# Tail tiles of four batches, seeded dots and one last store in a record-counting kernel

## The chip, the cores and the metric

The kernel runs on one core of a Trainium2 chip. The metric is the device time of one execution in microseconds (us).

Engines: DVE is VectorE, ACT is ScalarE, Pool is GpSimd, PE is TensorE, SP is SyncE (here it only issues transfers).

## The reference

```
x: (8, 2048, 4096) float32      w: (4096, 1) float32
proj = (x @ w).squeeze(-1)                      # (8, 2048)
cm = np.maximum.accumulate(proj, axis=1)
is_record = (proj >= cm).astype(np.float32)
return np.cumsum(is_record, axis=1)             # (8, 2048) float32
```

x is 268 MB and each element is used once.

## The kernel before

Positions 0 to 1919 are done in four groups. A group takes eight tiles, one for each batch, of 128 partitions with 4, 4, 4 and then 3 rows of x each. Of every row, DVE multiplies and sums 2816 columns (one custom instruction, "dot"); Pool multiplies the other 1280 and ACT sums these. The sum of a dot is written out by a second instruction, the "read-out". PE turns the sums into an (8, positions) layout, and DVE runs scan, compare and scan on it (running maximum, comparison with it, running count). The last 128 positions of all batches are the tail, in eight tiles (numbered 0 to 7) of 64 positions of 2 batches; tiles 6 and 7 are cut into column pieces, so that little work is left after the last landing. A tail tile holds several batches in its 128 partitions; "masking" multiplies its sums by a 0/1 pattern of the batches, so that a matmul puts each sum in the row of its batch.

```
H = 2; Q = P // H                  # batches in a tail tile, positions in it
LAST = [(B-2, 1696, D, (1696, VC), (VC, D)), (B-2, 0, 1696, (0, 1696), None),
        (B-1, 2592, D, (2592, CV), (CV, D)), ..., (B-1, 352, 736, (352, 736), None),
        (B-1, 0, 352, (0, 352), None)]      # tile, columns loaded, DVE's, Pool's

def dot(xsl, wsl, dst):
    return V.tensor_tensor_reduce(out=xsl, in0=xsl, in1=wsl, scale=1.0, scalar=0.0,
                                  op0=ALU.mult, op1=ALU.add, accum_out=dst)

def group_dots(r, g=0):                               # DVE
    for t in range(B):
        if r == R:
            V.wait_ge(xs[t], 16).then_inc(go, 1)      # landed: DVE tells Pool
        for j in range(r):
            i = dot(...)
            if j == 0 and r < R:
                i._wait_ge(xs[t], 16).then_inc(go, 1) # last group
            elif j == 1:
                i.then_inc(xs[t], -16)
# [cut] Pool: first product of each tile waits for go >= 1

# the end of the tail
for j in range(NP):
    sums(i, accs[:, j:j+1], accs[:, NP+j:NP+j+1])     # five pieces of tile 7
V.wait_ge(pa, na)
V.tensor_reduce(out=fin, in_=accs, op=ALU.add, ...)   # add the pieces' sums
by_batch(B-1, fin, False, True, sd, nv).then_inc(psr, 1)   # mask on DVE, matmul
tail_scans(EARLY, B, ...)                             # last 64 positions
SY.dma_start(out=out[:, S0:], in_=cnt_l)._wait_ge(cs, NG+3).then_inc(oe, 16)
G.wait_ge(oe, 16 * 2)                                 # Pool waits for both stores
```

The last group's 384 columns are stored earlier, from the middle of the load queue; `cnt_l` holds the tail's 128 columns, 4 KB.

Of the kernel before, what the change touches and what calls it, by code (L numbers as in the profile page):

```python
# [20 lines left out]
def kernel(  # L21
# [16 lines left out]
    P = 128  # L38
# [17 lines left out]
    H = 2  # L56
    Q = P // H
    LAST = [
        (B - 2, 1696, D, (1696, VC), (VC, D)),
        (B - 2, 0, 1696, (0, 1696), None),  # L60
        (B - 1, 2592, D, (2592, CV), (CV, D)),
        (B - 1, 1440, 2592, (1792, 2592), (1440, 1792)),
        (B - 1, 736, 1440, (736, 1280), (1280, 1440)),
        (B - 1, 352, 736, (352, 736), None),
        (B - 1, 0, 352, (0, 352), None),
    ]
    def rows_of(m):
        return m * H % B, m * H // B * Q

    TILES = [(m, 0, D, (0, VC), (VC, D)) for m in range(B - 2)] + LAST  # L70
    NP = sum(q[0] == B - 1 for q in LAST)
    EARLY = 4
    W2, W2C = 1280, WC
# [10 lines left out]
    small = sb([P, 352], "small")  # L84
    w2 = sb([P, W2C], "w2")
    xall = sb([P, NS * R * D], "xall")
# [4 lines left out]
    masked = sb([P, 2 * P], "masked")  # L91
    fold = sb([P, 2 * B - H + Q], "fold")
    cm_l, cnt_l = (sb([B, P], n) for n in ("cm_l", "cnt_l"))
# [3 lines left out]
    by_b, by_i = fold[:, : 2 * B - H], fold[:, 2 * B - H :]  # L97
# [3 lines left out]
    def cut(n):  # L101
        off[0] += n
        assert off[0] <= 352
        return small[:, off[0] - n : off[0]]

    sum_v, sum_p = cut(R * B), cut(R * B)
    acc_v, acc_p = cut(B + 1), cut(B)
    accs = cut(2 * NP)
    fin = cut(1)
# [4 lines left out]
    def sem(name):  # L114
# [5 lines left out]
    ws, bw, wc, cs, od, oe, psr, pd, pl, go, sd, pa, con, fo, ms, p7, mg = (  # L120
        sem(n) for n in "ws bw wc cs od oe psr pd pl go sd pa con fo ms p7 mg".split()
# [4 lines left out]
    def dot(xsl, wsl, dst):  # L126
        return V.tensor_tensor_reduce(  # L127
            out=xsl, in0=xsl, in1=wsl, scale=1.0, scalar=0.0,
            op0=ALU.mult, op1=ALU.add, accum_out=dst,
        )  # L130
# [35 lines left out]
    with tc.tile_critical(no_gpsimd_drain=True):  # L166
# [30 lines left out]
        for i, (m, c0, c1, _, _) in enumerate(TILES):  # L197
# [11 lines left out]
            if i == len(TILES) - 4:  # L209
                SY.dma_start(  # L210
                    out=out[:, STARTS[-1] : S0], in_=cnt[:, : S0 - STARTS[-1]]
                )._wait_ge(cs, NG + 1).then_inc(oe, 16)
# [9 lines left out]
        G.memset(by_b, 0.0).then_inc(con, 1)  # L222
# [5 lines left out]
        for n, k in enumerate(order):  # L228
# [17 lines left out]
            out=by_b[:, B - H : B], in_=identity.rearrange("p (i b) -> p b i", b=H),  # L246
# [12 lines left out]
        def group_dots(r, g=0):  # L259
            for t in range(B):  # L260
                b, xb = B - 1 - t, at(g, t)
                if r == R:
                    V.wait_ge(xs[t], 16).then_inc(go, 1)
                for j in range(r):
# [4 lines left out]
                    if j == 0 and r < R:  # L269
                        i._wait_ge(xs[t], 16).then_inc(go, 1)  # L270
                    elif j == 1:
                        i.then_inc(xs[t], -16)
# [10 lines left out]
        def group_products(r, g=0):  # L283
            for t in range(B):
                for j in range(r):
                    xl = at(g, t)[:, j * D + VC : (j + 1) * D]
                    i = G.tensor_mul(out=xl, in0=xl, in1=w_sb).then_inc(pl, 1)  # L287
                    if j == 0:
                        i._wait_ge(go, 1)
                G.sem_inc(go, -1)  # L290

        G.wait_ge(wc, 3)
        with G.Fori(0, NL):
            group_products(R)
        group_products(RS[-1], NL)
# [17 lines left out]
        def group_rows(r):  # L313
            T.wait_ge(fr[B - 1], 2).then_inc(p7, 1)
            T.sem_inc(fr[B - 1], -2)
            T.wait_ge(od, 16).then_inc(od, -16)  # L316
# [14 lines left out]
        nv = npool = na = nm = on_a = on_g = 0  # L331

        def sums(i, dst_v, dst_p):
# [3 lines left out]
            dot(xb[:, v[0] : v[1]], w_v[:, v[0] : v[1]], dst_v)._wait_ge(  # L337
# [12 lines left out]
        def by_batch(m, acc, start, stop, *wait):  # L350
            nonlocal nm, on_a, on_g
            e = masked[:, nm * B : (nm + 1) * B]
            b, q = rows_of(m)
            on = by_b[:, B - H - b : 2 * B - H - b]
            pool = m < B - 2 and wait[0] is sd
            if pool:
                G.tensor_tensor(
                    out=e, in0=on, in1=acc.to_broadcast([P, B]), op=ALU.mult
                )._wait_ge(*wait).then_inc(mg, 1)
            elif m < B - 1:  # L360
                A.activation(out=e, in_=on, func=ACTF.Copy, scale=acc)._wait_ge(  # L361
                    *wait
                ).then_inc(ms, 1)
            else:
                V.tensor_tensor(  # L365
                    out=e, in0=on, in1=acc.to_broadcast([P, B]), op=ALU.mult
                )._wait_ge(*wait).then_inc(ms, 1)
            nm += 1
            if pool:
                on_g += 1  # L370
            else:
                on_a += 1
            return T.matmul(  # L373
                out=ps[:B, q : q + Q], lhsT=e, rhs=by_i, start=start, stop=bool(stop),
            )._wait_ge(*((mg, on_g) if pool else (ms, on_a)))

        def tail_scans(m0, m1, cm0, cnt0, base):
            a, b = (m * H * Q // B for m in (m0, m1))
            scans(cm_l[:, a:b], cnt_l[:, a:b], ps[:B, a:b], cm0, cnt0, base)

        n = RS[-1] * P
        for i, (m, c0, _, _, p) in enumerate(TILES[: -NP]):
            dv = acc_v[:, i : i + 1]
            sums(i, dv, acc_p[:, m : m + 1])
            if m in (0, EARLY):
                T.wait_ge(cs, NG + 1 + (m > 0))
            if p:
                by_batch(m, acc_p[:, m : m + 1], rows_of(m)[0] == 0, False, pa, na)
# [50 lines left out]
```

## Time and profile before

| | before |
|---|---|
| time, median of 3 runs | 630.22 us (630.19 to 630.41) |
| span of the profiled run | 628.8 us |
| busy: DVE, Pool, ACT, PE | 65%, 59%, 29%, 5% |
| load queue's share of 16 DMA engines' span | 98.9% |
| HBM read | 268.45 MB, 427 GB/s over the span |

These are the page's lines on the DMA engines: busy tenths in 40 slices of the span, GB/s in the same slices, the load queue with its share of 16 engines' span, and the chain of waits by engine.

```profile
DMA  9999999999999999999999999999999999999996
GB/s 401 400 467 400 467 400 467 401 463 404 463 404 463 404 463 404 464 404 463 404 463 404 463 404 467 400 464 404 467 417 444 407 450 441 411 450 441 405 424 248
...
q1 hardware_dynamic: 6560, 268.50, 98.9%
...
POOL 52%; issue 38%; DMA 6%; PE 2%; DVE 1%; SPq 0%; POOLq 0%; ACT 0%; ACTq 0%
```

The DMA engines are 90% busy or more until the last slice. The GB/s line swings from slice to slice; the trace's packets are up to 64 KB long, but whether that is why was not tested. A full tile of 8.39 MB lands every 19.3 us, which is 435 GB/s. The Trainium skill, page "DMA: Bandwidth & Descriptors", section Specifications, gives 435 GB/s as the ceiling of the fabric; this trace sits on it. So the kernel is bound by its load stream, and only what lies before and after that stream can be saved. The chain's "POOL 52%" is no limit: the chain is followed back from tile to tile through whichever engine released the next step, while Pool itself is idle 41% of the span.

This is the end of the timeline of the kernel before: start in us, duration in us, engine, line, operation, output and inputs, shapes, and in brackets how long the engine was idle and what ended that.

```profile
623.39 0.55 DVE L127 CUSTOM_DVE_ANT_0 xall<-xall,w_v 128x384 f32<-128x384 f32 x1
...
623.87 0.52 DVE L127 CUSTOM_DVE_ANT_0 xall<-xall,w_v 128x352 f32<-128x352 f32 x1
624.31 0.08 DVE L127 DVE_READ_ACCUMULATOR2_ANT small<- 128x1 f32 x1
624.43 0.16 DVE L400 TENSOR_REDUCE small<-small 128x1 f32<-128x10 f32 x1
624.62 0.17 DVE L365 TENSOR_TENSOR masked<-fold,small 128x8 f32<-128x8 f32 x1
...
624.85 0.38 PE L373 MATMUL ps<-fold,masked 128*8 128x64 f32 x2 [2.46 <-DVE masked L365]
625.27 0.34 DVE L143 TENSOR_TENSOR_SCAN cm_l<-ps,cm_l,small 8x64 f32<-8x64 f32 x1 [0.48 <-PE ps L373]
625.64 0.22 DVE L146 TENSOR_TENSOR ps<-ps,cm_l 8x64 f32<-8x64 f32 x1
625.89 0.34 DVE L149 TENSOR_TENSOR_SCAN cnt_l<-ps,cnt_l,small 8x64 f32<-8x64 f32 x1
626.26 0.31 SPq L407 DMA_DIRECT2D out_dram<-cnt_l  x1
```

Read it as a chain without gaps: two last dots (384 and 352 columns), the second's read-out at 624.31, the reduce, the masking of the sums by batch, a matmul (which these traces record as two), scan, compare and scan over 64 positions, the store's issue at 626.26. No dot waits for a landing here: DVE is slightly late. From the store's issue to the end of the span, 2.56 us, no engine computes. (The page rounds spans to 0.1 us; the traces hold 628.817 for this kernel, and the times counted from an event below use the traces' nanoseconds, so they can differ by 0.01 from what the lines shown give.)

The DMA view of the same kernel, GB/s in 40 slices of 0.125 us from 625 to 630 us, shows that store's data: one slice.

```profile
GB/s 0 0 0 0 0 0 0 0 0 0 0 0 0 0 0 0 33 0 0 0 0 0 0 0 0 0 0 0 0 0 0 0 0 0 0 0 0 0 0 0
```

And two lines of its timeline from the last group of full tiles show when the two engines begin one and the same tile.

```profile
584.40 3.09 DVE L127 CUSTOM_DVE_ANT_0 xall<-xall,w_v 128x2816 f32<-128x2816 f32 x1 [5.41 <-DMA xall<-in_x_dram]
...
587.57 8.63 POOL L287 TENSOR_TENSOR xall<-xall,w_sb 128x1280 f32<-128x1280 f32 x3 [5.91 <-POOLq L290]
```

DVE begins on the landing, Pool 3.17 us later: there `go` is raised by DVE's first dot when it is done. In the groups of four rows DVE raises it by a separate wait, before the dot, and Pool begins with DVE.

### The profile page before, as it was taken

What the parts mean: (1) busy time and instruction counts of PE and PEld (TensorE: products, weight loads), DVE (VectorE), ACT (ScalarE), POOL (GpSimd) and SP (SyncE); (2) the same over time, 40 slices, a digit from 0 to 9 for tenths busy, and PEclk for the clock granted to TensorE, in tenths of its full rate; (3) what the DMA queues carried; (4) which work ended last, traced back from release to release, by engine and by line L of the source; (5) the groups of instructions that cost most, each with busy time, mean ns of one, the idle gap of its engine ahead of it and who ended that gap; (6) DMA issues with size and microseconds to landing.
All of it is one profiled execution on the core that took longest, in us unless ns stands there. A gap on an engine that the chain in (4) does not pass through costs nothing.

```text
span 628.8 us, 1182 instructions
## 1 busy us (share of the span) xinstructions
PE 31.7 (5%) x108; PEld 15.0 (2%) x108; DVE 406.9 (65%) x292; ACT 180.4 (29%) x273; POOL 369.9 (59%) x147
## 2 busy tenths in 40 slices
PE   8000000000010000000010000000002000000031
PEld 3000000000010000000010000000001000000010
DVE  0755776556785557755579555676556966655897
ACT  1222332223322233222233222332223232232353
POOL 0555676446765557745567555676555666666685
PEclk9999999999965555555555555555555555555555
DMA  9999999999999999999999999999999999999996
GB/s 401 400 467 400 467 400 467 401 463 404 463 404 463 404 463 404 464 404 463 404 463 404 463 404 467 400 464 404 467 417 444 407 450 441 411 450 441 405 424 248
DMA packets 6579, 268.55 MB, mean 427 GB/s; under 512 B 768, under 2 KB 1040, under 8 KB 1584
## 3 DMA queue, kind: packets, MB, share of 16 engines
q1 hardware_dynamic: 6560, 268.50, 98.9%
q10 hardware_dynamic: 16, 0.02, 0.0%
q14 instruction: 3, 0.02, 0.0%
HBM read 268.45 MB, written 0.07 MB: 427 GB/s over the span
## 4 chain that ended last, share of the span: by engine, by line
POOL 52%; issue 38%; DMA 6%; PE 2%; DVE 1%; SPq 0%; POOLq 0%; ACT 0%; ACTq 0%
POOL xall L287 52%; DMA xall<-in_x_dram 6%; PE w_v L231 2%; DVE xall L127 0%; PE ps L231 0%; DMA w<-in_w_dram 0%; SPq L199 0%; POOLq L290 0%; ACT w L242 0%; PE ps L373 0%; DVE cm_l L143 0%; DVE cnt_l L149 0%; DVE ps L146 0%; ACT xall L133 0%; DVE masked L365 0%
## 5 line engine op out<-in xcount | busy, mean ns | idle before, releaser
L127 DVE CUSTOM_DVE_ANT_0 xall<-xall,w_v 128x2816 f32<-128x2816 f32 (+3 forms) x133 | 388.5, 2973 | 186.4 <-DMA xall<-in_x_dram 186.4
L287 POOL TENSOR_TENSOR xall<-xall,w_sb 128x1280 f32<-128x1280 f32 x120 | 344.7, 2904 | 249.4 <-POOLq L290 249.4
L133 ACT ACTIVATE xall<-xall 128x1280 f32<-128x1280 f32 (+1 forms) x130 | 162.8, 1252 | 428.2 <-POOL xall L287 415.8
L319 PE MATMUL ps<-identity,small 128*8 128x128 f32 x60 | 13.1, 407 | 570.8 <-PEq L316 570.8
L133 ACT ACTIVATION_READ_ACCUMULATOR xall<-xall 128x1 f32 x130 | 24.2, 186 | 0.0
L343 POOL TENSOR_TENSOR xall<-xall,w_sb 128x1280 f32<-128x1280 f32 (+1 forms) x8 | 21.6, 2702 | 2.5 <-DMA xall<-in_x_dram 2.5
L319 PEld LDWEIGHTS ps<-identity,small 128*8 128x8 f32 x60 | 7.4, 126 | 577.6 <-issue 573.6
L143 DVE TENSOR_TENSOR_SCAN cm<-ps,cm,small 8x512 f32<-8x512 f32 (+1 forms) x5 | 6.1, 1217 | 14.0 <-PE ps L319 14.0
L231 PE MATMUL w_v<-w,identity 8*128 8x512 f32 x14 | 12.2, 1056 | 0.0
L127 DVE DVE_READ_ACCUMULATOR2_ANT small<- 128x1 f32 x133 | 10.8, 81 | 0.0
L253 DVE MEMSET ps<- 8x512 f32 x1 | 0.5, 485 | 15.7 <-ACT w L242 15.7
L149 DVE TENSOR_TENSOR_SCAN cnt<-ps,cnt,small 8x512 f32<-8x512 f32 (+1 forms) x5 | 6.1, 1217 | 0.2
L373 PE MATMUL ps<-fold,masked 128*8 128x64 f32 x32 | 4.6, 305 | 19.9 <-ACT masked L361 13.0
L231 PEld LDWEIGHTS w_v<-w,identity 8*128 8x128 f32 x14 | 4.7, 333 | 7.3 <-issue 7.3
L239 ACT COPY w_sb<-w_v 128x768 f32<-128x768 f32 x1 | 0.8, 798 | 11.4 <-PE w_v L231 11.4
L146 DVE TENSOR_TENSOR ps<-ps,cm 8x512 f32<-8x512 f32 (+1 forms) x5 | 3.3, 660 | 0.2
L373 PEld LDWEIGHTS ps<-fold,masked 128*8 128x8 f32 x32 | 2.5, 113 | 22.2 <-ACT masked L361 14.4
L361 ACT ACTIVATE masked<-fold,small 128x8 f32<-128x8 f32 x9 | 2.5, 297 | 0.2
L231 PE MATMUL ps<-w,identity 8*128 8x512 f32 x2 | 2.1, 1136 | 2.9 <-DMA w<-in_w_dram 2.9
L238 ACT ACT_TABLE_LOAD x1 | 1.3, 1283 | 2.7 <-DVE fold L249 2.7
L245 DVE TENSOR_REDUCE fold<-identity 128x2 f32<-128x128 f32 x1 | 0.3, 285 | 2.2 <-POOL cnt L224 2.2
L343 POOL TENSOR_TENSOR xall<-xall,w 128x352 f32<-128x352 f32 (+1 forms) x2 | 1.5, 732 | 0.2 <-DMA xall<-in_x_dram 0.2
(23 smaller groups left out, 7.0 us busy)
## 6 DMA issues: line engine op xcount, KB each, us to landing
xall<-in_x_dram SPq DMA_DIRECT2D x8, 6144.0 KB, 30.4
xall<-in_x_dram SPq DMA_DIRECT2D x6, 2048.0 KB, 39.3
xall<-in_x_dram SPq DMA_DIRECT2D x1, 1200.0 KB, 33.3
xall<-in_x_dram SPq DMA_DIRECT2D x1, 848.0 KB, 34.8
xall<-in_x_dram SPq DMA_DIRECT2D x1, 752.0 KB, 36.0
xall<-in_x_dram SPq DMA_DIRECT2D x1, 576.0 KB, 36.8
xall<-in_x_dram SPq DMA_DIRECT2D x24, 44.9
xall<-in_x_dram SPq DMA_DIRECT2D x1, 352.0 KB, 17.3
```

The lines of the kernel that those rows point to most:

```text
L127: return V.tensor_tensor_reduce(out=xsl, in0=xsl, in1=wsl, scale=1.0, scalar=0.0, op0=ALU.mult, op1=ALU.add, accum_out=dst,)
L133: return A.activation(out=xsl, in_=xsl, func=ACTF.Copy, accum_out=dst)
L143: V.tensor_tensor_scan(out=cm_, data0=src, data1=low, initial=cm0, op0=ALU.max, op1=ALU.max,)._wait_ge(psr, base).then_inc(psr, 1)
L146: V.tensor_tensor(out=src, in0=src, in1=cm_, op=ALU.is_ge)._wait_ge(psr, base + 1).then_inc(psr, 1)
L149: V.tensor_tensor_scan(out=cnt_, data0=src, data1=low, initial=cnt0, op0=ALU.add, op1=ALU.max,)._wait_ge(psr, base + 2).then_inc(cs, 1)
L231: i = T.matmul(out=dst, lhsT=identity[:NW, k : k + 1].to_broadcast([NW, P]), rhs=w_row, start=True, stop=True,).then_inc(bw, 1)
L238: A.copy(out=w_sb[:, CV - VC :], in_=ps)._wait_ge(bw, 1).then_inc(wc, 1)
L287: i = G.tensor_mul(out=xl, in0=xl, in1=w_sb).then_inc(pl, 1)
L319: i = T.matmul(out=ps[:B, j : r * P : r], lhsT=l[:, j * B : (j + 1) * B], rhs=identity, start=k == 0, stop=k == 1,)
L343: G.tensor_mul(out=xl, in0=xl, in1=w_pool(*p))._wait_ge(xq[i], 16).then_inc(pl, 1)
L361: A.activation(out=e, in_=on, func=ACTF.Copy, scale=acc)._wait_ge(*wait).then_inc(ms, 1)
L373: return T.matmul(out=ps[:B, q : q + Q], lhsT=e, rhs=by_i, start=start, stop=bool(stop),)._wait_ge(*((mg, on_g) if pool else (ms, on_a)))
```

## The change

The intent: tail tiles of 32 positions of 4 batches, so that the scans and the matmuls after the last landing are over 32 positions and not 64; pieces' sums carried from dot to dot as the seed of the accumulation, so that no reduce is needed; one last store in place of two; Pool waiting for landings itself and not for DVE. The tail's counts go into the last columns of `cm` and `cnt`, so that one store covers the last group and the tail, 8 rows of 2 KB. ACT, not Pool, waits for it.

```
-    H = 2
+    H = 4
     LAST = [
-        (B - 2, 1696, D, (1696, VC), (VC, D)),      ... 7 pieces, the last two 384 and 352 wide
+        (B - 2, 1568, D, (1568, 3296), (3296, D)),
+        (B - 2, 0, 1568, (0, 928), (928, 1568)),
+        (B - 1, 2464, D, (2464, 3360), (3360, D)),
+        (B - 1, 1632, 2464, (1632, 2464), None),
+        (B - 1, 960, 1632, (960, 1376), (1376, 1632)),
+        (B - 1, 480, 960, (480, 960), None),
+        (B - 1, 0, 480, (0, 480), None),
     ]
+    SEED = (None, 0, None, None, 2, 3, 4)
-    def dot(xsl, wsl, dst):
+    def dot(xsl, wsl, dst, seed=0.0):
-            out=xsl, in0=xsl, in1=wsl, scale=1.0, scalar=0.0,
+            out=xsl, in0=xsl, in1=wsl, scale=1.0, scalar=seed,
-            if i == len(TILES) - 4:                  # store of 384 columns in the load queue
-                SY.dma_start(out=out[:, STARTS[-1] : S0], in_=cnt[...])._wait_ge(cs, NG + 1)...
-                if r == R:
-                    V.wait_ge(xs[t], 16).then_inc(go, 1)
-                    if j == 0 and r < R:
-                        i._wait_ge(xs[t], 16).then_inc(go, 1)
-                    elif j == 1:
-                        i.then_inc(xs[t], -16)
+                    if j == 0:
+                        i._wait_ge(xs[t], 16)
-                        i._wait_ge(go, 1)            # Pool
-                G.sem_inc(go, -1)
+                        i._wait_ge(xs[t], 16)        # Pool
             group_products(R)
+            G.wait_ge(pg, 1).then_inc(pg, -1)
+            if r == R:                               # PE, at the end of a group
+                for s in xs:
+                    T.sem_inc(s, -16)
+                T.sem_inc(pg, 1)
[cut: masks of 4 columns, the tail's loop]
-        V.wait_ge(pa, na)
-        V.tensor_reduce(out=fin, in_=accs, ...)
+        pick(V, col(9, 1), v)._wait_ge(sd, nv).then_inc(ml, 1)
+        T.wait_ge(cs, NG + 3)
+        turn(6, ...); turn(7, ...); turn(8, ...)     # from ACT, ACT and Pool
+        turn(9, 3, False, True)._wait_ge(ml, 1).then_inc(psr, 1)
+        tail_scans(3, 4, 10)
-        SY.dma_start(out=out[:, S0:], in_=cnt_l)._wait_ge(cs, NG + 3).then_inc(oe, 16)
-        G.wait_ge(oe, 16 * 2)
+        SY.dma_start(out=out[:, STARTS[-1] :], in_=cnt)._wait_ge(cs, NG + 4).then_inc(oe, 16)
+        A.wait_ge(oe, 16)
```

More of the change, by code (lines that the diff above doesn't have):

```diff
@@ L53 @@
     CV = 3584
-    H = 2
+    H = 4
     Q = P // H
     LAST = [
-        (B - 2, 1696, D, (1696, VC), (VC, D)),
-        (B - 2, 0, 1696, (0, 1696), None),
-        (B - 1, 2592, D, (2592, CV), (CV, D)),
-        (B - 1, 1440, 2592, (1792, 2592), (1440, 1792)),
-        (B - 1, 736, 1440, (736, 1280), (1280, 1440)),
-        (B - 1, 352, 736, (352, 736), None),
-        (B - 1, 0, 352, (0, 352), None),
+        (B - 2, 1568, D, (1568, 3296), (3296, D)),
[5 more added lines that the diff above has]
+        (B - 1, 0, 480, (0, 480), None),
     ]
+    SEED = (None, 0, None, None, 2, 3, 4)
     def rows_of(m):
@@ L70 @@
     TILES = [(m, 0, D, (0, VC), (VC, D)) for m in range(B - 2)] + LAST
-    NP = sum(q[0] == B - 1 for q in LAST)
-    EARLY = 4
-    W2, W2C = 1280, WC
+    W2, W2C = 928, 736
     pool = ctx.enter_context(tc.tile_pool(name="sb", bufs=1))
@@ L83 @@
     identity = sb([P, P], "identity")
-    small = sb([P, 352], "small")
     w2 = sb([P, W2C], "w2")
+    small = sb([P, 128], "small")
     xall = sb([P, NS * R * D], "xall")
@@ L90 @@
     cnt = sb([B, N], "cnt")
-    masked = sb([P, 2 * P], "masked")
-    fold = sb([P, 2 * B - H + Q], "fold")
-    cm_l, cnt_l = (sb([B, P], n) for n in ("cm_l", "cnt_l"))
+    masked = sb([P, 10 * B], "masked")
+    fold = sb([P, H + Q], "fold")
     w_v = wpool.tile([P, CV], FP32, name="w_v")
@@ L96 @@
     w_row = w2[:NW, :WC]
-    by_b, by_i = fold[:, : 2 * B - H], fold[:, 2 * B - H :]
+    by_b, by_i = fold[:, :H], fold[:, H:]
     off = [0]
@@ L102, in cut @@
         off[0] += n
-        assert off[0] <= 352
+        assert off[0] <= 128
         return small[:, off[0] - n : off[0]]
     sum_v, sum_p = cut(R * B), cut(R * B)
-    acc_v, acc_p = cut(B + 1), cut(B)
-    accs = cut(2 * NP)
-    fin = cut(1)
+    acc_v, acc_p = cut(B - 2), cut(B - 2)
+    part_v, part_p = cut(len(LAST)), cut(len(LAST))
     neg = cut(1)[:B]
@@ L119 @@
     xq = [sem("xq") for _ in TILES]
-    ws, bw, wc, cs, od, oe, psr, pd, pl, go, sd, pa, con, fo, ms, p7, mg = (
-        sem(n) for n in "ws bw wc cs od oe psr pd pl go sd pa con fo ms p7 mg".split()
+    ws, bw, wc, cs, od, oe, psr, pd, pl, go, sd, pa, con, fo, ms, p7, mg, pg, ml = (
+        sem(n) for n in "ws bw wc cs od oe psr pd pl go sd pa con fo ms p7 mg pg ml".split()
     )
     V, A, G, T, SY = nc.vector, nc.scalar, nc.gpsimd, nc.tensor, nc.sync
-    def dot(xsl, wsl, dst):
+    def dot(xsl, wsl, dst, seed=0.0):
         return V.tensor_tensor_reduce(
-            out=xsl, in0=xsl, in1=wsl, scale=1.0, scalar=0.0,
+            out=xsl, in0=xsl, in1=wsl, scale=1.0, scalar=seed,
             op0=ALU.mult, op1=ALU.add, accum_out=dst,
@@ L208 @@
                 d._wait_ge(*free(u, NG))
-            if i == len(TILES) - 4:
-                SY.dma_start(
-                    out=out[:, STARTS[-1] : S0], in_=cnt[:, : S0 - STARTS[-1]]
-                )._wait_ge(cs, NG + 1).then_inc(oe, 16)
         G.memset(identity, 0.0).then_inc(con, 1)
@@ L221 @@
         G.memset(neg, NEG)._wait_ge(con, 3).then_inc(con, 1)
-        G.memset(by_b, 0.0).then_inc(con, 1)
+        G.memset(masked, 0.0).then_inc(con, 1)
         G.memset(cm[:, N - 1 :], NEG).then_inc(con, 1)
@@ L245 @@
         V.tensor_reduce(
-            out=by_b[:, B - H : B], in_=identity.rearrange("p (i b) -> p b i", b=H),
+            out=by_b, in_=identity.rearrange("p (i b) -> p b i", b=H),
             op=ALU.add, axis=mybir.AxisListType.X,
@@ L328, with sums @@
         group_rows(RS[-1])
-        nv = npool = na = nm = on_a = on_g = 0
-        def sums(i, dst_v, dst_p):
+        nv = npool = na = 0
+        def sums(i, dst_v, dst_p, seed=0.0):
             nonlocal nv, npool, na
@@ L336, in sums @@
             xb = slot(m)[1]
-            dot(xb[:, v[0] : v[1]], w_v[:, v[0] : v[1]], dst_v)._wait_ge(
+            dot(xb[:, v[0] : v[1]], w_v[:, v[0] : v[1]], dst_v, seed)._wait_ge(
                 xq[i], 16
@@ L348, in sums @@
                 na += 1
-        def by_batch(m, acc, start, stop, *wait):
-            nonlocal nm, on_a, on_g
-            e = masked[:, nm * B : (nm + 1) * B]
-            b, q = rows_of(m)
-            on = by_b[:, B - H - b : 2 * B - H - b]
-            pool = m < B - 2 and wait[0] is sd
-            if pool:
-                G.tensor_tensor(
-                    out=e, in0=on, in1=acc.to_broadcast([P, B]), op=ALU.mult
-                )._wait_ge(*wait).then_inc(mg, 1)
-            elif m < B - 1:
-                A.activation(out=e, in_=on, func=ACTF.Copy, scale=acc)._wait_ge(
-                    *wait
-                ).then_inc(ms, 1)
-            else:
-                V.tensor_tensor(
-                    out=e, in0=on, in1=acc.to_broadcast([P, B]), op=ALU.mult
-                )._wait_ge(*wait).then_inc(ms, 1)
-            nm += 1
-            if pool:
-                on_g += 1
-            else:
-                on_a += 1
-            return T.matmul(
-                out=ps[:B, q : q + Q], lhsT=e, rhs=by_i, start=start, stop=bool(stop),
-            )._wait_ge(*((mg, on_g) if pool else (ms, on_a)))
@@ L377, in tail_scans @@
-        def tail_scans(m0, m1, cm0, cnt0, base):
-            a, b = (m * H * Q // B for m in (m0, m1))
-            scans(cm_l[:, a:b], cnt_l[:, a:b], ps[:B, a:b], cm0, cnt0, base)
-        n = RS[-1] * P
-        for i, (m, c0, _, _, p) in enumerate(TILES[: -NP]):
-            dv = acc_v[:, i : i + 1]
-            sums(i, dv, acc_p[:, m : m + 1])
-            if m in (0, EARLY):
-                T.wait_ge(cs, NG + 1 + (m > 0))
-            if p:
-                by_batch(m, acc_p[:, m : m + 1], rows_of(m)[0] == 0, False, pa, na)
-            mm = by_batch(m, dv, False, rows_of(m)[0] + H == B and c0 == 0, sd, nv)
-            if i == 2:
-                group_scans(RS[-1])
-            if m == EARLY - 1:
-                mm.then_inc(psr, 1)
-            if m == EARLY:
-                tail_scans(0, EARLY, cm[:, n - 1 : n], cnt[:, n - 1 : n], 4)
@@ L396 @@
-        for j in range(NP):
-            i = len(TILES) - NP + j
-            sums(i, accs[:, j : j + 1], accs[:, NP + j : NP + j + 1])
-        V.wait_ge(pa, na)
-        V.tensor_reduce(
-            out=fin, in_=accs, op=ALU.add, axis=mybir.AxisListType.X
-        )._wait_ge(sd, nv).then_inc(sd, 1)
-        nv += 1
-        by_batch(B - 1, fin, False, True, sd, nv).then_inc(psr, 1)
-        ne = EARLY * H * Q // B
-        tail_scans(EARLY, B, cm_l[:, ne - 1 : ne], cnt_l[:, ne - 1 : ne], 7)
@@ L407, with col, pick, pick_a @@
-        SY.dma_start(out=out[:, S0:], in_=cnt_l)._wait_ge(cs, NG + 3).then_inc(oe, 16)
-        G.wait_ge(oe, 16 * 2)
+        def col(n, m=0):
+            return masked[:, n * B + m % 2 * H : n * B + m % 2 * H + H]
+        def pick(eng, e, acc):
+            return eng.tensor_tensor(
+                out=e, in0=by_b, in1=acc.to_broadcast([P, H]), op=ALU.mult
+            )
+        def pick_a(e, acc):
+            return A.activation(
+                out=e, in_=by_b, func=ACTF.Copy, scale=acc
+            )._wait_ge(pa, na).then_inc(ms, 1)
@@ new lines, in turn, with tail_scans @@
+        def turn(n, k, start, stop):
+            return T.matmul(
+                out=ps[:B, k * Q : (k + 1) * Q], lhsT=masked[:, n * B : (n + 1) * B],
+                rhs=by_i, start=start, stop=stop,
+            )
+        def tail_scans(k0, k1, base):
+            c = S0 - STARTS[-1]
+            a, b = k0 * Q, k1 * Q
+            scans(
+                cm[:, c + a : c + b], cnt[:, c + a : c + b], ps[:B, a:b],
+                cm[:, c + a - 1 : c + a], cnt[:, c + a - 1 : c + a], base,
+            )
@@ new lines @@
+        for m in range(B - 2):
+            k = m // 2
+            v, p = acc_v[:, m : m + 1], acc_p[:, m : m + 1]
+            sums(m, v, p)
+            pick_a(col(2 * k, m), p)
+            pick(G, col(2 * k + 1, m), v)._wait_ge(sd, nv).then_inc(mg, 1)
+            if m == 2:
+                group_scans(RS[-1])
+            if m == 4:
+                tail_scans(0, 2, 4)
+            if m % 2:
+                if k != 1:
+                    T.wait_ge(cs, NG + 1 + k // 2)
+                turn(2 * k, k, True, False)._wait_ge(ms, m + 1)
+                mm = turn(2 * k + 1, k, False, True)._wait_ge(mg, m + 1)
+                if k:
+                    mm.then_inc(psr, 1)
@@ new lines @@
+        npart = [0, 0]
+        for i in range(B - 2, len(TILES)):
+            n = i - (B - 2)
+            m, p = TILES[i][0], TILES[i][4]
+            z = m - (B - 2)
+            v, dp = part_v[:, n : n + 1], part_p[:, n : n + 1]
+            s = SEED[n]
+            if s is not None:
+                V.wait_ge(sd, B - 2 + s + 1)
+            sums(i, v, dp, 0.0 if s is None else part_v[:, s : s + 1])
+            if p:
+                pick_a(col(6 + npart[z], m), dp)
+                npart[z] += 1
+            if n in (1, len(LAST) - 2):
+                pick(G, col(8, m), v)._wait_ge(sd, nv).then_inc(mg, 1)
+            if n == 1:
+                tail_scans(2, 3, 7)
@@ new lines @@
+        assert npart == [2, 2]
+        pick(V, col(9, 1), v)._wait_ge(sd, nv).then_inc(ml, 1)
+        T.wait_ge(cs, NG + 3)
+        turn(6, 3, True, False)._wait_ge(ms, B - 2 + 3)
+        turn(7, 3, False, False)._wait_ge(ms, B - 2 + 4)
+        turn(8, 3, False, False)._wait_ge(mg, B)
+        turn(9, 3, False, True)._wait_ge(ml, 1).then_inc(psr, 1)
+        tail_scans(3, 4, 10)
+        SY.dma_start(out=out[:, STARTS[-1] :], in_=cnt)._wait_ge(cs, NG + 4).then_inc(
+            oe, 16
+        )
```

## The prediction

> **What bounds the kernel now.** The load stream of x. In the 40 slices the DMA engines are 90% busy until the last, and the queue table gives the load queue 98.9% of 16 engines' span. Full tiles (8.39 MB) land every 19.3 us, 435 GB/s. The Trainium skill, "DMA: Bandwidth & Descriptors", Specifications, gives a fabric ceiling of 435 GB/s: this trace sits on it. DVE (65%), Pool (59%) and ACT (29%) wait for landings. So only the ends count, above all from the last landing (about 623.6 us: issued 606.7, 16.9 to landing) to the end at 628.8.
>
> **The exposed end (timeline).** DVE is 0.25 us behind the landings: last dot (352 columns) 623.87, read out at 624.39, reduce 624.43, masking 624.62, 64-column matmul 624.85 to 625.24, scan, compare, scan 625.27 to 626.23 (0.34, 0.22, 0.34), store issued 626.26, end 628.8.
>
> **What the change does there.**
> - No reduce: minus 0.19 us. Seeds are two dots old, so their waits should be met.
> - Scans over 32, not 64: a scan takes 0.34 us at 64 columns, 1.27 at 512, so 2.1 ns a column; the compare 1.0. Minus 0.17 us for three.
> - Matmul over 32 columns (407 ns at 128, 305 at 64): minus 0.05 us.
> - Last piece 480 wide, not 352: plus 0.13 us (1.04 ns a column), but DVE is about on time at it and starts 0.25 us earlier.
> - The extra 32-column scans come before the third piece, where I work out DVE free by 620.35 and the landing at 620.44: hidden.
> - New risk: the last piece with a Pool share (256 columns, landing about 622.3) goes through Pool (2.1 ns a column), ACT (0.86, plus 0.5 us of read and masking), both behind a 736-column share, then three matmuls in order: masking done near 624.4, last matmul near 625.05. This, not DVE, may end last, and eats half the gain.
> - One store of 16 KB instead of 4: plus 0.05 us; the 2.2 us from its issue to the end stay.
> Sum: 0.3 us less, at most 0.6.
>
> **Off the critical path.** Pool waiting on landings: it already starts 0.03 us before DVE at each tile and idles 7.8 us. Nine more semaphore steps on PE at group ends delay scans that wait for landings anyway. Clears at the head hide under the first load (to 23 us). Without the store in the queue the last three loads can be issued before 605.47, into a queue 17 us deep: nothing.
>
> **Four-batch loads.** Row pieces stay whole. The skill's page (section "Why a DMA increments its semaphore by 16 and not by 1") takes the engine count from the slowest dimension: 64 becomes 32, both give 16. Tail tiles now land every 4.87 us (2.1 MB, 431 GB/s); I expect the same. One per cent on the tail's 39 us would be 0.4 us, as large as the gain.
>
> **Prediction.** 629.85 us, 8 in 10 between 629.2 and 630.4. Faster by over 2%: 0.005; within 2%: 0.99; slower: 0.005.
>
> **What would show it.** Full tiles every 19.3 us; tail tiles every 4.9; last landing within 0.2 us of 623.6 and the last dot starting at it; no reduce; last scans near 0.27, 0.19, 0.27 us; the span ending 0.3 us sooner. If ACT's last masking ends after DVE's, the risk is real.
>
> **What would make it wrong.** Four-batch loads at another rate; seeded dots waiting for seeds or costing more; the larger store landing later; a stall at group boundaries from Pool's new wait that leaves the queue dry.

## The result

The changed kernel took 630.52 us (median of 6 runs, 630.05 to 631.05); the kernel before in the same rounds took 630.4 us (median of 6, 630.19 to 631.1). The ratio is 1.0000, with a 95% interval of 0.9987 to 1.0013: the same.

Run again later on another chip (run e12 below), the changed kernel took 630.25 us against 630.47, ratio 0.9996 (0.9982 to 1.0009). Again the same, and the forecast gain of 0.3 us (0.05%) is smaller than either interval. The traces must show what became of it.

The lines of the changed kernel's page that answer to those above:

```profile
DMA  9999999999999999999999999999999999999996
...
q1 hardware_dynamic: 6544, 268.50, 98.9%
...
DMA 16%; POOL 3%; DVE 2%; issue 1%; PE 1%; ACT 0%; SPq 0%
```

The stream is as full as before. The chain of waits is now put down to "DMA 16%" and hardly to Pool, because Pool waits for landings directly; nothing about the limit has changed. This shows how little the share of an engine in the chain says when everything follows one stream.

The end of the changed kernel's timeline:

```profile
623.65 0.71 DVE L124 CUSTOM_DVE_ANT_0 xall<-xall,w_v,small 128x480 f32<-128x480 f32 x1
...
624.29 0.71 DVE L124 CUSTOM_DVE_ANT_0 xall<-xall,w_v,small 128x480 f32<-128x480 f32 x1
...
624.58 0.30 ACT L352 ACTIVATE masked<-fold,small 128x4 f32<-128x4 f32 x1
624.92 0.08 DVE L124 DVE_READ_ACCUMULATOR2_ANT small<- 128x1 f32 x1
...
624.93 0.60 PE L357 MATMUL ps<-fold,masked 128*8 128x32 f32 x6 [0.45 <-ACT masked L352]
625.04 0.16 DVE L347 TENSOR_TENSOR masked<-fold,small 128x4 f32<-128x4 f32 x1
625.57 0.27 DVE L140 TENSOR_TENSOR_SCAN cm<-ps,cm,small 8x32 f32<-8x32 f32 x1 [0.37 <-PE ps L357]
625.87 0.19 DVE L143 TENSOR_TENSOR ps<-ps,cm 8x32 f32<-8x32 f32 x1
626.10 0.27 DVE L146 TENSOR_TENSOR_SCAN cnt<-ps,cnt,small 8x32 f32<-8x32 f32 x1
626.39 0.32 SPq L413 DMA_DIRECT2D out_dram<-cnt  x1
```

The last two dots are 480 wide and carry a third input, the seed in `small`. There is no reduce; the scans take 0.27, 0.19 and 0.27 us. The PE line holds three matmuls of two records each, of which the first begins after ACT's masking (624.58) and the last after DVE's (625.04).

The DMA view of the changed kernel, GB/s in slices of 0.125 us from 625 to 630 us:

```profile
GB/s 0 0 0 0 0 0 0 0 0 0 0 0 0 0 0 0 0 66 49 17 0 0 0 0 0 0 0 0 0 0 0 0 0 0 0 0 0 0 0 0
```

The store's data now take three slices, not one. And the same last-group tile as above:

```profile
585.00 3.09 DVE L124 CUSTOM_DVE_ANT_0 xall<-xall,w_v 128x2816 f32<-128x2816 f32 x1 [5.40 <-DMA xall<-in_x_dram]
585.05 8.64 POOL L276 TENSOR_TENSOR xall<-xall,w_sb 128x1280 f32<-128x1280 f32 x3 [5.88 <-DMA xall<-in_x_dram]
```

Pool begins 0.05 us after DVE, 3.1 us sooner against DVE than before.

### Where the time went

The two profiled runs cannot be subtracted from end to end: their streams ran differently. Full tiles landed 19.3 us apart, but in each trace a few took longer, up to 20.2 us, most of them in the first 150 us and not the same ones. The start of DVE's last dot of full width (2816 columns, tail tile 5), which begins within 0.03 us of its tile's landing in every run, lay at 613.56 us before and at 614.15 us in the changed kernel, and in all 14 profiled runs between 613.08 and 614.15. So the tables below count from that start, which takes the stream's spread out. Last landings come from the trace's landing records.

| from that start to, us | before | changed | changed again (e12) |
|---|---|---|---|
| last landing | 10.03 | 9.95 | 9.94 |
| start of the last dot | 10.31 | 10.14 | 10.10 |
| start of DVE's masking | 11.07 | 10.89 | 10.86 |
| first of the last scans | 11.71 | 11.42 | 11.38 |
| issue of the last store | 12.70 | 12.24 | 12.21 |
| end of the span | 15.26 | 15.10 | 15.07 |
| store's issue to the end | 2.56 | 2.86 | 2.86 |

Up to the store's issue the change gains 0.46 to 0.49 us, more than the 0.35 us that the prediction's sum leaves before the store. After it, it gives back 0.30 us, where the prediction said 0.05. What remains is 0.16 to 0.19 us, about half of the forecast 0.3. The kernel before was profiled once; against e7 below, whose tail is the same code and which ended at 15.20, it is 0.10 to 0.13 us.

### The profile page after: what moved, and what is told of

Read it like the earlier page. It is cut to its first block, busy times and chain, and to the rows that moved or that the text cites. A ratio compares the mean times of both kernels' runs of the same rounds, so it can differ in the third digit from the quotient of the medians. Undisturbed runs are those within 1.5% of the kernel's fastest.

```text
span 629.3 us, 1140 instructions
## 1 busy us (share of the span) xinstructions
PE 29.1 (5%) x96; PEld 13.5 (2%) x96; DVE 407.3 (65%) x294; ACT 181.2 (29%) x274; POOL 370.7 (59%) x149
## 3 DMA queue, kind: packets, MB, share of 16 engines
q1 hardware_dynamic: 6544, 268.50, 98.9%
## 5 line engine op out<-in xcount | busy, mean ns | idle before, releaser
L124 DVE CUSTOM_DVE_ANT_0 xall<-xall,w_v 128x2816 f32<-128x2816 f32 (+1 forms) x129 | 385.5, 3041 | 181.8 <-DMA xall<-in_x_dram 181.8
L130 ACT ACTIVATE xall<-xall 128x1280 f32<-128x1280 f32 (+2 forms) x130 | 162.9, 1253 | 428.6 <-POOL xall L276 408.3
L336 POOL TENSOR_TENSOR xall<-xall,w_sb 128x1280 f32<-128x1280 f32 (+2 forms) x8 | 21.1, 2632 | 3.1 <-DMA xall<-in_x_dram 3.0
L140 DVE TENSOR_TENSOR_SCAN cm<-ps,cm,small 8x512 f32<-8x512 f32 (+3 forms) x8 | 7.0, 869 | 18.8 <-PE ps L312 18.4
L146 DVE TENSOR_TENSOR_SCAN cnt<-ps,cnt,small 8x512 f32<-8x512 f32 (+3 forms) x8 | 7.0, 870 | 0.3
L143 DVE TENSOR_TENSOR ps<-ps,cm 8x512 f32<-8x512 f32 (+3 forms) x8 | 3.9, 487 | 0.3
L124 DVE CUSTOM_DVE_ANT_0 xall<-xall,w_v,small 128x480 f32<-128x480 f32 (+2 forms) x4 | 3.1, 810 | 0.2 <-DVE small L124 0.2
L357 PE MATMUL ps<-fold,masked 128*8 128x32 f32 x20 | 2.0, 235 | 25.3 <-ACT masked L352 17.7
L352 ACT ACTIVATE masked<-fold,small 128x4 f32<-128x4 f32 x10 | 3.0, 298 | 0.3
L336 POOL TENSOR_TENSOR xall<-xall,w 128x640 f32<-128x640 f32 (+1 forms) x2 | 2.3, 1137 | 0.1
```

Of the source, the lines that this page charges most:

```text
L130: return A.activation(out=xsl, in_=xsl, func=ACTF.Copy, accum_out=dst)
L140: V.tensor_tensor_scan(out=cm_, data0=src, data1=low, initial=cm0, op0=ALU.max, op1=ALU.max,)._wait_ge(psr, base).then_inc(psr, 1)
L143: V.tensor_tensor(out=src, in0=src, in1=cm_, op=ALU.is_ge)._wait_ge(psr, base + 1).then_inc(psr, 1)
L146: V.tensor_tensor_scan(out=cnt_, data0=src, data1=low, initial=cnt0, op0=ALU.add, op1=ALU.max,)._wait_ge(psr, base + 2).then_inc(cs, 1)
L336: G.tensor_mul(out=xl, in0=xl, in1=w_pool(*p))._wait_ge(xq[i], 16).then_inc(pl, 1)
L352: return A.activation(out=e, in_=by_b, func=ACTF.Copy, scale=acc)._wait_ge(pa, na).then_inc(ms, 1)
```

## The experiments

The theory after the first comparison, S: the larger last store takes 0.3 us longer to land. The rival, R: the longer end comes from the engine that waits for it (ACT in place of Pool), or is chance. Further questions were whether the four-batch loads, the seeds and Pool's own wait had cost or gained something that the sum hides, and whether ACT's last masking or DVE's ends the tail. Twelve kernels ran. All times of the second table stand after the descriptions.

### e1: the store taken apart again

The changed kernel with 384 columns stored in the load queue as before, 128 columns (4 KB) at the end.

```
+            if i == len(TILES) - 4:
+                SY.dma_start(out=out[:, STARTS[-1]:S0], in_=cnt[:, :S0-STARTS[-1]])._wait_ge(cs, NG+1).then_inc(oe, 16)
-        SY.dma_start(out=out[:, STARTS[-1]:], in_=cnt)...;  A.wait_ge(oe, 16)
+        SY.dma_start(out=out[:, S0:], in_=cnt[:, S0-STARTS[-1]:])...;  A.wait_ge(oe, 32)
```

> The changed kernel with its one 16 KB store taken apart again: 384 columns in the load queue as before, 128 columns (4 KB) at the end. Theory S (the large store lands later): from the issue of the last store to the end of the span about 2.55 us, as in the kernel before, instead of 2.9; from the last tile's start on DVE to the end 0.3 us less than in the changed kernel; time 0.3 us under the changed kernel's. Rival R (the end is later because ACT, not Pool, waits for the store, or by chance): stays at 2.8 to 2.9 us.

Issue to end was 2.61 us, so 0.25 of the 0.30 us came back; 0.05 did not. From the reference start to the end it was 14.81 us, 0.29 less than in the changed kernel, as expected. Issue to end is counted from 625.823 to the span's end at 628.433.

Time 630.04 us against 630.64 before, ratio 0.9990 (0.9976 to 1.0004), unresolved. S holds for most of it, not for all.

### e2: 480 columns early, 32 at the end

```
+        c = S - Q - STARTS[-1]
+        SY.dma_start(out=out[:, STARTS[-1]:S-Q], in_=cnt[:, :c])._wait_ge(cs, NG+3).then_inc(oe, 16)
+        SY.dma_start(out=out[:, S-Q:], in_=cnt[:, c:])._wait_ge(cs, NG+4).then_inc(oe, 16);  A.wait_ge(oe, 32)
```

> The changed kernel with 480 columns stored when the third quarter of the tail is scanned and only 32 columns (1 KB) at the end. Theory S: issue to end 2.5 us or a little less, about as in e1; if the cost goes with bytes, at most 0.06 us under e1. Risk: 15 KB are stored while the last loads land, which may delay these by up to 0.3 us, so that the time gains nothing over the changed kernel. Rival R: 2.8 to 2.9 us.

Issue to end 2.55 us, 0.06 under e1. The feared delay did not come: the last landing lay 9.95 us after the reference start, as in the changed kernel, although 15 KB were being stored at the time. Time 629.93 us, ratio 0.9991 (0.9978 to 1.0005).

### e3: the kernel before with one large store

```
-    cm_l, cnt_l = (sb([B, P], n) for n in ("cm_l", "cnt_l"))
+    cm_l, cnt_l = (t[:, RS[-1]*P:] for t in (cm, cnt))
-    [the store of 384 columns in the load queue]
-        SY.dma_start(out=out[:, S0:], in_=cnt_l)...;  G.wait_ge(oe, 32)
+        SY.dma_start(out=out[:, STARTS[-1]:], in_=cnt)...;  G.wait_ge(oe, 16)
```

> The kernel before with the tail's scans in the last columns of cm and cnt and one 16 KB store at the end, nothing else changed; Pool still waits for the store. Theory S: issue to end goes from 2.55 to about 2.85 us, and the time 0.3 us up. Rival R: stays at 2.55 us.

Issue to end 2.79 us: up 0.23, with Pool still waiting. It is counted from the issue at 625.926 to the span's end at 628.713. The DMA view shows the store's data, GB/s in 40 slices of 0.125 us from 625 us:

```profile
GB/s 0 0 0 0 0 0 0 0 0 0 0 0 0 49 66 17 0 0 0 0 0 0 0 0 0 0 0 0 0 0 0 0 0 0 0 0 0 0 0 0
```

The data spread over three slices, as in the changed kernel. The run time (630.5 us, ratio 1.0003, 0.9989 to 1.0017) cannot resolve it.

### e6: Pool waits for the large store

The changed kernel with one edit: `A.wait_ge(oe, 16)` becomes `G.wait_ge(oe, 16)`.

> The changed kernel with Pool instead of ACT waiting for the last store. Theory S: issue to end stays at 2.8 to 2.9 us (at most 0.07 us less, the part that the store's landing does not explain). Rival R: it falls to 2.55 us.

Issue to end 2.82 us: 0.04 less. Time 630.31 us, ratio 0.9994 (0.9980 to 1.0008). Together with e1 and e3 this makes a square of two sizes and two waiting engines, every profiled run with its own value:

| last store, issue to end, us | Pool waits | ACT waits |
|---|---|---|
| 4 KB | 2.56, 2.54, 2.57 (before, e4, e7) | 2.61, 2.62 (e1, e8) |
| 16 KB | 2.79, 2.82 (e3, e6) | 2.86 in each (changed, e5, e10, e12) |

Sixteen KB cost 0.23 to 0.25 us more than four in either column, and the column with ACT is 0.06 us longer on the mean in either row. The two sum to the 0.30 us. But the columns do not differ in the engine alone. Where only the engine differs (the changed kernel and e6, e2 and e11 below) ACT costs 0.04 us: from the store's last landing to the start of Pool's clearing of the semaphores it takes 0.71 to 0.72 us when Pool waits and 0.75 to 0.76 when ACT does. The other 0.02 us is that clearing itself: 0.31 us in before, e3 and e4, and 0.33 in all other runs. e7 shows it with Pool waiting and only the edits to the semaphores, one of which is new, so it goes with these and not with ACT. R, as far as it put all of it down to the engine, falls. That ACT's wait is longer is shown; why is not.

### e4: four-batch tail tiles alone

The kernel before with `H = 2` made `H = 4` and nothing else.

> The kernel before with tail tiles of 32 positions of 4 batches and nothing else. My account: the loads run at the same rate (tail tiles land every 4.85 to 4.9 us), only the matmuls get narrower (64 to 32 columns): the last pair 0.38 to 0.3 us, the end at most 0.1 us earlier. Rival (the layout costs load time and hides a gain): tail tiles land every 4.92 us or more, or the time from the first tail tile to the last landing is at least 0.3 us longer.

Tail tiles landed 4.86 us apart before, in e4 and in the changed kernel. From the landing of tail tile 0 to the last landing it took 34.36 us both in the kernel before (two batches) and in e4 (four), so the layout costs no load time. The gain at the end is the narrower matmul, as two lines of e4's timeline show:

```profile
624.17 0.17 DVE L365 TENSOR_TENSOR masked<-fold,small 128x8 f32<-128x8 f32 x1
...
624.71 0.34 DVE L143 TENSOR_TENSOR_SCAN cm_l<-ps,cm_l,small 8x64 f32<-8x64 f32 x1 [0.37 <-PE ps L373]
```

From DVE's masking to the scan it took 0.54 us in place of 0.64 us (624.62 to 625.27 in the lines of before, which are rounded): 0.11 us, twice the predicted 0.05. Time 630.15 us, ratio 0.9996 (0.9982 to 1.0010).

### e5: no seeds

```
-            if s is not None:
-                V.wait_ge(sd, B - 2 + s + 1)
-            sums(i, v, dp, 0.0 if s is None else part_v[:, s : s + 1])
+            sums(i, v, dp)
```

> The changed kernel with all seeds 0 and without the waits for them: a wrong result on purpose (parts of the last two tiles' sums are missing). My account: a seeded dot costs 0.06 us more than an unseeded one of its width, so the last 480-column dot takes 0.58 us from issue to issue instead of 0.64, three of them give 0.1 to 0.2 us at the end, and the second piece no longer waits 0.15 us for the first's sum, which the wait for the third piece's landing hides. Last masking on DVE 0.1 to 0.2 us earlier. Rival (seeds are free): the same durations.

The arithmetic is wrong, since parts of the sums of the last 32 positions of each batch are missing; the output still agreed with the reference, which says only that the counts hardly depend on these sums. The end of its timeline:

```profile
623.48 0.65 DVE L124 CUSTOM_DVE_ANT_0 xall<-xall,w_v 128x480 f32<-128x480 f32 x1
...
624.05 0.65 DVE L124 CUSTOM_DVE_ANT_0 xall<-xall,w_v 128x480 f32<-128x480 f32 x1
...
624.47 0.30 ACT L352 ACTIVATE masked<-fold,small 128x4 f32<-128x4 f32 x1
624.63 0.08 DVE L124 DVE_READ_ACCUMULATOR2_ANT small<- 128x1 f32 x1
624.74 0.16 DVE L347 TENSOR_TENSOR masked<-fold,small 128x4 f32<-128x4 f32 x1
...
625.35 0.27 DVE L140 TENSOR_TENSOR_SCAN cm<-ps,cm,small 8x32 f32<-8x32 f32 x1 [0.45 <-PE ps L357]
```

Against the changed kernel's lines: the last dot's read-out comes 0.58 us after its start in place of 0.64, and dot follows dot in the same times. The other seeded dots lose as much without their seeds (928 columns: 1.11 to 1.05 us; 416 columns: 0.57 to 0.51), while the dot of 832 columns, unseeded in both, takes 0.95 us in both. So a seed held in memory costs about 0.06 us a dot. DVE's masking comes 10.70 us after the reference start, 0.16 to 0.19 us sooner. But the scan came only 0.08 to 0.11 us sooner, at 11.31: its idle time before it grew to 0.45 us from 0.37, because ACT's masking (624.47) and the matmuls behind it on PE now end last: DVE's masking is done 0.11 us before the last of these begins. Time 630.72 us, ratio 0.9998 (0.9984 to 1.0011): unresolved.

### e7: Pool waits on landings, alone

The kernel before with only the semaphore edits of the change: DVE no longer raises `go`, Pool's first product waits on `xs[t]`, PE lowers `xs` and raises `pg` at the end of each group.

> The kernel before with Pool waiting on landings itself, nothing else. My account: in the groups of four rows nothing changes; in the last group Pool starts each tile 3 us sooner (its start came with the end of DVE's first dot, not with the landing as the prediction said), and the time stays the same within 0.2 us, because the queue never runs dry. Rival (buffers freed 3 us sooner let the loads run sooner): landings of the tail tiles move up, and the time falls by 0.3 us or more.

The same last-group tile in e7's timeline:

```profile
584.17 3.09 DVE L127 CUSTOM_DVE_ANT_0 xall<-xall,w_v 128x2816 f32<-128x2816 f32 x1 [5.41 <-DMA xall<-in_x_dram]
584.21 8.63 POOL L283 TENSOR_TENSOR xall<-xall,w_sb 128x1280 f32<-128x1280 f32 x3 [5.88 <-DMA xall<-in_x_dram]
```

In the last group Pool begins with DVE, 3.1 us sooner than before. Nothing downstream moved: tail tiles 4.86 us apart, the last landing 10.02 us after the reference start (before 10.03), the end 15.20 after it. Time 630.7 us against 630.34, ratio 1.0003 (0.9989 to 1.0017). The rival is refuted: buffers freed sooner bring nothing; the load queue's share is 98.8% here and 98.9% before.

### e8: more for Pool and ACT

As e1, with the fifth piece's split moved: `(960, 1376), (1376, 1632)` becomes `(960, 1312), (1312, 1632)`.

> As e1, and 64 columns of the fifth last piece moved from DVE to Pool and ACT (416 and 256 become 352 and 320). If DVE ends the tail: last masking on DVE 0.07 us sooner than e1's, ACT's last masking 0.2 us later and still before it; 0.4 us under the changed kernel and 0.4 us under the kernel before. If ACT ends it: the last matmul later by 0.1 us or more.

A miss: DVE's masking came 10.84 us after the reference start, as in e1. DVE's last pieces in e8's timeline:

```profile
622.41 0.58 DVE L124 CUSTOM_DVE_ANT_0 xall<-xall,w_v,small 128x352 f32<-128x352 f32 x1
...
622.97 0.71 DVE L124 CUSTOM_DVE_ANT_0 xall<-xall,w_v,small 128x480 f32<-128x480 f32 x1
...
624.36 0.16 DVE L351 TENSOR_TENSOR masked<-fold,small 128x4 f32<-128x4 f32 x1
```

The dot of 352 columns is 0.06 us shorter, as meant, but the next dot then starts at 622.97, not when the read-out at 622.92 begins: it waits for its piece to land. ACT's last masking ended 0.07 us later than e1's, not 0.2. So moving work away from the dots before that piece can gain no more than DVE lags behind the landing of the second last piece: 0.05 us in e1, where the store in the queue makes the pieces land later, and 0.11 to 0.14 us in the changed kernel, where the split was not tried. Time 630.12 us, ratio 0.9991 (0.9978 to 1.0005).

### e9 and e10: where the store's rows lie

The changed kernel, with the last store's source replaced. Their outputs are wrong, which doesn't matter for the times. In e9 the eight rows are every fourth partition from 0 to 28 (`in_=w_sb[0:32:4, : S - STARTS[-1]]`); e10 is its control, partitions 0 to 7 (`w_sb[0:8, ...]`). The idea, theory P: the Trainium skill, page "SBUF — State Buffer", section "Door 1: The DMA port swizzle", says that partitions 0 to 3 share one of 16 DMA ports and 4 to 7 another, and gives 27.2 GB/s for a port. An estimate from this page: 12 KB more over two ports take 12,288 bytes / 54.4 GB/s = 0.23 us, which is what the square above shows (0.24).

> The changed kernel, but the last store takes its 16 KB from eight rows of w_sb, every fourth partition from 0 to 28: a wrong result on purpose. Theory P (the store is slow because its rows lie in neighbouring partitions that share DMA ports): the data phase shrinks from 0.3 us to about 0.1, and issue to end falls from 2.86 us to 2.6 or 2.65. Rival (the bytes cost, wherever they lie): 2.86 us as in the changed kernel.

> The control for e9: the same wrong source, but partitions 0 to 7 as cnt has them. Both theories: 2.86 us from issue to end, as in the changed kernel; anything else means that the source tile matters and e9 tells nothing.

e10 met its expectation, 2.86 us. e9 took 3.25 us, so the expectation of the total was missed, in the wrong direction. First e10's, then e9's issue (start, duration), and after each the store's data, GB/s in slices of 0.1 us from 625 us:

```profile
625.42 0.32 SPq L413 DMA_DIRECT2D out_dram<-w_sb  x1
```

```profile
GB/s 0 0 0 0 0 0 0 0 0 0 0 0 102 41 21 0 0 0 0 0 0 0 0 0 0 0 0 0 0 0 0 0 0 0 0 0 0 0 0 0
```

```profile
625.28 0.76 SPq L413 DMA_DIRECT2D out_dram<-w_sb  x1
```

```profile
GB/s 0 0 0 0 0 0 0 0 0 0 0 0 0 0 0 0 123 41 0 0 0 0 0 0 0 0 0 0 0 0 0 0 0 0 0 0 0 0 0 0
```

The data phase did as P says. In e10 the eight packets of 2 KB took 81 to 233 ns each in the trace's packet records, in e9 81 ns each, and they fill two slices in place of three. But the issue took 0.76 us in place of 0.32, and by the packet records the data began 1.39 us after the issue's start and not 0.79. So here a source with a step over partitions (one run each) costs more to issue than its faster data give back. P is supported for the data phase; as a way to save time it fails. The single run times were 630.37 us (e9) and 630.11 us (e10), within the spread of the other kernels.

### e11 and e12: a version for both kernels, and the changed kernel again

e11 is e2 with `G.wait_ge(oe, 32)`; e12 is the changed kernel, unedited.

> e2 with Pool instead of ACT waiting for the stores, as a version that might beat both kernels. Store sizes and the waiting engine add up: issue to end 2.48 to 2.49 us (e2: 2.55, less 0.065); from the start of the last full dot to the end 14.70 us (before: 15.26, changed: 15.10). Time 0.5 us under the kernel before and 0.4 under the changed one, if the load stream takes its median time.

> The changed kernel itself, for the spread of its profile and a comparison with e11 on the same chip: issue to end 2.86 us, from the start of the last full dot to the end 15.1 us; time within 0.3 us of the kernel before.

e11: issue to end 2.52 us (expected 2.48 to 2.49), the end 14.74 us after the reference start (expected 14.70): in the trace 0.5 us sooner than the kernel before and 0.33 to 0.36 sooner than the changed one. Time 629.88 us (629.64 to 630.0) against 630.47 before, ratio 0.9990 (0.9976 to 1.0004). All its five runs lie below all nine of the kernel before in that call (630.2 to 630.79), but the interval holds 1, so no run time here proves it. e12: 2.86 us and 15.07 us, time 630.25, as expected.

All profiled runs, counted from the start of the last dot of full width:

| run | last landing | DVE's masking | first of the last scans | store's issue | issue to end | end |
|---|---|---|---|---|---|---|
| before | 10.03 | 11.07 | 11.71 | 12.70 | 2.56 | 15.26 |
| changed | 9.95 | 10.89 | 11.42 | 12.24 | 2.86 | 15.10 |
| e1 | 10.01 | 10.84 | 11.38 | 12.20 | 2.61 | 14.81 |
| e2 | 9.95 | 10.87 | 11.40 | 12.23 | 2.55 | 14.78 |
| e3 | 9.98 | 10.97 | 11.61 | 12.60 | 2.79 | 15.39 |
| e4 | 10.03 | 11.02 | 11.56 | 12.55 | 2.54 | 15.09 |
| e5 | 9.95 | 10.70 | 11.31 | 12.13 | 2.86 | 14.99 |
| e6 | 9.95 | 10.87 | 11.40 | 12.22 | 2.82 | 15.04 |
| e7 | 10.02 | 10.99 | 11.63 | 12.63 | 2.57 | 15.20 |
| e8 | 10.01 | 10.84 | 11.37 | 12.19 | 2.62 | 14.81 |
| e9 | 9.94 | 10.85 | 11.38 | 12.21 | 3.25 | 15.46 |
| e10 | 9.95 | 10.90 | 11.43 | 12.25 | 2.86 | 15.11 |
| e11 | 9.94 | 10.86 | 11.39 | 12.22 | 2.52 | 14.74 |
| e12 | 9.94 | 10.86 | 11.38 | 12.21 | 2.86 | 15.07 |

Rows with the same code up to the store (changed, e2, e6, e11, e12; or before and e7, whose tails are the same) show how well this repeats: within 0.08 us.

## Why the prediction was right or wrong

The class (within 2%) was right by what is bounded here: the stream of 268 MB fills the span, and only 5 us at the end could change. A forecast of no change would have done as well. The first median, 630.52, lies 0.1 us over the range (629.2 to 630.4 for a single figure of 629.85), but the kernel before took 630.4 in those rounds and not the 630.22 that the forecast started from; the ratio of 1.0000 on 630.22, and the 630.25 of e12, lie within it. A ratio of 0.9994 was forecast; the intervals hold both. That the net gain came within 0.2 us of the forecast is in part luck: the gain before the store was larger than forecast by 0.1 us, the loss after it by 0.25 us. Point by point:

- **Bound by the load stream: right.** DMA share 98.9% before and after; full tiles 19.3 us apart, tail tiles 4.86. Four-batch loads kept the rate (e4), which agrees with the section of the Trainium skill that the prediction drew on ("DMA: Bandwidth & Descriptors", "Why a DMA increments its semaphore by 16 and not by 1"): the slowest dimension of 32 still gives 16 engines. The trace has 16 landing records for each of these loads.
- **No reduce, minus 0.19 us: right.** From the last dot's read-out to the masking it took 0.32 us before and 0.12 after.
- **Shorter scans, minus 0.17 us: right.** The time from the first scan to the store's issue went from 0.99 to 0.83 us.
- **Narrower matmul, minus 0.05 us: too small.** e4 alone gave 0.11 us.
- **The last dot, on time at its landing: nearly.** The last dot began 0.28 us after the last landing before (0.22 in e7), and 0.16 to 0.18 after it in the changed kernel: gained 0.03 to 0.12, not 0.25. Its own length, start to read-out, grew by 0.20 us (0.44 to 0.64), not by 0.13. Unseeded, the same 480 columns take 0.58 us (e5), so the 0.13 for the width was right and the rest is the seed: 0.06 us a dot, where the prediction had them free and only listed "costing more" among the dangers. "Seeds are two dots old" was wrong for the second piece, whose seed is the dot just before it; DVE waited 0.15 us there, but then waited for the third piece's landing anyway.
- **The new risk, ACT ends last: not met, but close.** ACT's last masking ended at 10.73 us of the table's clock, DVE's at 11.05. With DVE sooner by 0.19 us (e5) it is ACT's branch that ends last. Without the half that the risk was to eat, the prediction's terms before the store sum to 0.53 us, nearer to the 0.46 to 0.49 measured.
- **The store, plus 0.05 us and the rest "stays": the step that failed in size.** Issue to end grew by 0.30 us: 0.24 for 16 KB in place of 4 (e1, e3), 0.04 for ACT in place of Pool as the waiter (e6) and 0.02 for the longer clearing of semaphores (e7), two terms that the prediction did not have. It gave no working for its 0.05; at the loads' 435 GB/s, 12 KB would take 0.03 us. But the rows of the store lie in eight neighbouring partitions, and the data phase shows them sharing a far lower rate (e9 against e10): with 16 KB it lasts 0.31 us, with 4 KB 0.09, and with 16 KB from rows four partitions apart 0.14.
- **Taking the store out of the queue, nothing: slightly wrong.** In the runs with the 12 KB store among the loads the last landing lay at 10.01 to 10.03 us, in those without it at 9.94 to 9.98: 0.03 to 0.09 us (0.05 where only the store differs, e3 against before), part of what the changed kernel gains.
- **Pool's own wait, off the critical path: right, on a wrong reading.** "It already starts 0.03 us before DVE at each tile" is true of the groups of four rows only (0.05 us there); in the last group Pool was 3.17 us late before. e7 shows that this was worth nothing.
- **Semaphore steps on PE delay only scans that can wait: right.** First the kernel before, then the changed one, last read-out of ACT in a group and PE's first matmul after it:

```profile
481.10 0.19 ACT L133 ACTIVATION_READ_ACCUMULATOR xall<-xall 128x1 f32 x1
...
481.73 3.57 PE L319 MATMUL ps<-identity,small 128*8 128x128 f32 x16 [151.01 <-PEq L316]
```

```profile
481.66 0.19 ACT L130 ACTIVATION_READ_ACCUMULATOR xall<-xall 128x1 f32 x1
...
483.69 2.72 PE L312 MATMUL ps<-identity,small 128*8 128x128 f32 x12 [151.06 <-PEq L309]
```

PE starts 0.44 us after the end of ACT's last work before (481.10 + 0.19 to 481.73), and 1.84 us after it in the changed kernel. The nine steps cost about 1.4 us at this group's end, and neither landings nor the end show it. e7, which has only these edits, shows the same (1.80 to 1.85 us at its three group ends), and in the traces the nine instructions follow one another every 0.15 us.

What stays open: why ACT's wait for the last store ends 0.04 us later than Pool's, and why Pool's clearing of the semaphores takes 0.02 us longer with the change; why some full tiles of every run take up to 0.9 us longer, on which the spread of the run times rests; and whether e11's 0.5 us would hold in run times, which would take many more runs.

## What to carry to other kernels

When a stream fills the span, price a change at its end from the last landing to the end of the span, and count every step there, the last store too: it is a serial step like the others, and its bytes can cost several times what the load stream's rate says when its rows sit in few neighbouring partitions. Store what is ready while the loads still run and leave the smallest possible piece for the end. Where run times scatter more than the effect, measure from an event that comes from the stream itself, as the start of a given dot on its landing, and use the runs only to see that the sum does not contradict it.

## What the Trainium skill lacked or had wrong

- "DMA: Bandwidth & Descriptors", section "Anatomy of one DMA", gives a fixed part of about 2.0 us plus bytes over 436 GB/s (a fit for another issuing path). For a store from eight neighbouring partitions the slope here is far steeper: 12 KB more cost 0.24 us, where that formula gives 0.03. "SBUF — State Buffer" has the rule that explains the size (two ports, 0.23 us), but neither section says that a kernel's small last store is where it bites.
- No page seen gives the cost of issuing a store whose source steps over partitions: 0.76 us in place of 0.32 for eight rows of 2 KB.
- No page seen says that the engine that waits for the last store matters: ACT 0.04 us later than Pool.
- No page seen gives the cost of a seed held in memory for a multiply-and-accumulate on DVE: 0.06 us a dot.
- No page seen prices semaphore instructions of their own on PE between blocks of matmuls: about 1.4 us for nine, 0.15 us each.
